# A ring of six weight blocks and four landing buffers instead of seven and two, and adaLN work moved by a step

## The chip, the cores and the metric

The kernel runs on one core of a Trainium2 chip. The metric is the device time of one execution in microseconds, the median over runs. The core has these engines, each with its own queue that it works through in order: TensorE (PE, matmuls; PEld are its weight loads), VectorE (DVE), ScalarE (ACT), GpSimd (POOL) and SyncE (SP, which here only issues loads and stores). Data comes from HBM by DMA into SBUF; matmul results land in PSUM.

## The reference

Two layers of a diffusion backbone on 384 tokens of width 1024 (256 latent, 128 context), all in float32. A layer is a half-step SwiGLU feed-forward, a token mixing stage, and a second half-step feed-forward:

```python
x = x + 0.5 * post(swiglu(pre(x, 0), gate1, up1, down1), 0)
y = token_mix(pre(x, 1), ...)   # w_mix_in, four head groups, w_mix_out
x = x + post(y, 1)
x = x + 0.5 * post(swiglu(pre(x, 2), gate2, up2, down2), 2)
# pre(y, i)  = rms_norm(y) * norm_pre  * (1 + scale_i) + shift_i
# post(y, i) = gate_i * rms_norm(y) * norm_post
# shift, scale, gate = columns of silu(cond) @ w_ada + b_ada   (9 vectors of 1024 a layer, for two conds)
```

The token mixing projects to 2560 columns, which four groups share: a gated convolution of width 3 (A), differential attention (B), a convolution of width 31 with layer norm (C), and grouped-query attention with q/k norm (D). Their outputs go through one output projection.

## The kernel before, in words

**Precision by three products.** Each float32 operand is split into a high part (rounded to fp32r) and a low part (the rest), and a product is made of three matmuls: high by high, high by low, low by high (`mm3_a`, `mm3_b`, and the three in `rows_out`, L576 to L578). The third-order product is left out.

**The weight stream.** All weights but w_ada are packed on the host into 322 blocks of 128 x 1024 (one of 128 x 512), in the order of their use. The class `Stream` brings them in. `load` issues a block's DMA from SyncE into a landing buffer (`st`, pool `sp`, `STAGES` buffers). `pump` splits the next block: a cast by ScalarE (L167) into the high half of a ring slot (`wu`, pool `up`, `UNITS` slots), and a subtraction by VectorE (L168) into the low half; this frees the landing buffer, and `pump` asks for loads up to `STAGES` blocks ahead. `take(n)` hands out the next n blocks, and first pumps up to `first + UNITS`, `first` being the first block taken; with `ahead=False` it pumps only what it takes; `tick` pumps one more. A slot is free again when TensorE has read its block for the last time.

**The stages.** `ffn` first projects one or two column groups with tokens as rows (`take(4)`, `proj_b`, bank `ps_gu`; in the very first call in four quarters, together with the first adaLN), turns them by transposes (`ps_ht`), then loops over the other column groups with features as rows (two `take(2)` a step, 48 matmuls of 128x384 each, `ps_f`), and ends in `rows_out`: 22 down-projection blocks, 18 matmuls of 128x512 a block, the last `TAIL` = 4 taken together so that one token tile after the other finishes. Behind each token tile come the norms of `post` and of the next stage's `pre` (`xn`, transposes `ps_t`). `mix` begins with `take(4)` for group C, `take(4)` for group D (followed by `d_rows`, a chain of VectorE and GpSimd work for each token tile), then attention units with fill work between them: the first fill is `take(4, False)` for q and k of group B.

**adaLN.** The columns of shift, scale and gate for later stages are computed inside `ffn` by the class `Ada`, one object for 1024 columns (a unit). Its eight steps each load 128 rows of w_ada (`ast`, pool `ap_`, 2 buffers) and add them, weighted, to two accumulators on VectorE (L275, L279). `finish` then sums over partitions by ones-matmuls (`ps_ada`, L291); for shift and scale ScalarE copies the sums to `rows` (L297) and TensorE transposes them (`ps_mod`, L300); for a gate GpSimd loads bias and norm rows and writes the result out. The closure `more` in `ffn` makes the steps: at each half of a column group `max(len(adas) * ADA_J, 0.5)` of them, in `rows_out` at every second block so many that all are done by block `ADA_END`, where `more(100)` does what is left. The first call has six units, the others 4, 5 and 1.

**What sets the order.** The program is written in one order; a planner of the framework then lays out each engine's queue, by that order and by when it reckons that an operation's inputs are there. So matmuls of a later line can stand ahead of a transpose, and loads run ahead of the line that they are written in. On the chip each queue is worked through in order, with waits.

Of the kernel before, what the change touches and what calls it, by code (L numbers as in the profile page):

```python
# [12 lines left out]
F32 = mybir.dt.float32  # L13
# [6 lines left out]
P = 128  # L20
D = 1024
KC = D // P
# [7 lines left out]
CK = 31  # L30
CPAD = CK // 2
SK = 3
UNITS = 7
STAGES = 2
TAIL = 4
MOD_DVE = (2, 0)
ORDERS = ((0, 1, 2), (0, 1, 2))
# [7 lines left out]
NORM_GAP = 2  # L45
FIRST_T = 1
ADA_J = 0.28
ADA_END = 18
CONV1 = 4
A_STEPS = 11  # L50
MIX_ORDER = (6, 7, 0, 1, 4, 5, 2, 3)
# [135 lines left out]
def kernel(ctx: ExitStack, tc: tile.TileContext, a: dict):  # L187
    nc = tc.nc
# [19 lines left out]
    def mbank(name):  # L208
        return psp.tile([P, 512], F32, tag="msc", name=name, bufs=2)
# [3 lines left out]
    def nm(s):  # L213
        uid[0] += 1
        return f"{s}{uid[0]}"
# [41 lines left out]
    class Ada:  # L257


        def __init__(self, l, i, m):  # L260
            self.key = (l, i)
            self.m = m
            self.src = a["w_ada"][l, :, (3 * i + m) * D : (3 * i + m + 1) * D]
            self.k = 0

        def step(self, pool):
            k = self.k
            w = ap_.tile([P, D], F32, tag="ast", name=nm("ast"))
            nc.sync.dma_start(out=w, in_=self.src[k * P : (k + 1) * P, :])
            if k == 0:  # L270
                self.acc = [pool.tile([P, D], F32, tag="acc", name=nm("acc"), bufs=2) for _ in range(2)]
            for c in range(2):
                s1 = sc[:, k, 0, c : c + 1]
                if k == 0:
                    nc.vector.tensor_scalar(  # L275
                        out=self.acc[c], in0=w, scalar1=s1, scalar2=None, op0=ALU.mult
                    )
                else:
                    nc.vector.scalar_tensor_tensor(  # L279
                        out=self.acc[c], in0=w, scalar=s1, in1=self.acc[c], op0=ALU.mult, op1=ALU.add  # L280
                    )
            self.k += 1
            return self.k == KC

        def finish(self):
            l, i = self.key
            ps = mbank(nm("ps_ada"))
            for c in range(2):
                for h in range(2):
                    j = 2 * c + h  # L290
                    nc.tensor.matmul(  # L291
                        ps[32 * j : 32 * j + 32, :], lhsT=ones, rhs=self.acc[c][:, h * 512 : (h + 1) * 512],
                        start=True, stop=True, tile_position=(0, 32 * j),
                    )
            if self.m < 2:
                rows = tp.tile([P, 512], F32, tag="t2k", name=nm("rows"), bufs=4)
                nc.scalar.copy(out=rows, in_=ps)  # L297
                pt = mbank(nm("ps_mod"))
                for q in range(4):
                    nc.tensor.transpose(  # L300
                        pt[:, q * P : (q + 1) * P], rows[:, q * P : (q + 1) * P], ident
                    )
                if self.m == 0:
                    raws[(l, i)] = sm.tile([P, 2, KC, 2], F32, tag="mraw", name=nm("mraw"), bufs=2)
                raw = raws[(l, i)]
                pv = pt.rearrange("p (q c h r) -> p h q c r", q=4, c=2, h=2)
                for h in range(2):
                    nc.vector.tensor_copy(
                        out=raw[:, self.m, 4 * h : 4 * h + 4, :], in_=pv[:, h, :, :, 0]
                    )  # L310
                if self.m == 1:
                    A, B = modulation(l, i, raws.pop((l, i)), 0, KC)
                    mods[(l, i)] = [(A[:, 4 * q : 4 * q + 4], B[:, 4 * q : 4 * q + 4]) for q in range(2)]
            else:
                br = tp.tile([P, 512], F32, tag="t2k", name=nm("brow"), bufs=4)
                pr = tp.tile([P, 512], F32, tag="t2k", name=nm("prow"), bufs=4)
                for j in range(4):
                    h = j % 2
                    nc.gpsimd.dma_start(
                        out=br[32 * j : 32 * j + 32, :],  # L320
                        in_=a["b_ada"][l, (3 * i + 2) * D + h * 512 : (3 * i + 2) * D + (h + 1) * 512].partition_broadcast(32),
                    )
                    nc.gpsimd.dma_start(
                        out=pr[32 * j : 32 * j + 32, :],
                        in_=a["norm_post"][l, i, h * 512 : (h + 1) * 512].partition_broadcast(32),
                    )
                grow = tp.tile([P, 512], F32, tag="grow", name=nm("grow"))
                nc.vector.tensor_tensor(out=br, in0=br, in1=ps, op=ALU.add)
                nc.vector.scalar_tensor_tensor(  # L329
                    out=grow, in0=br, scalar=(1.0 if i == 1 else 0.5), in1=pr, op0=ALU.mult, op1=ALU.mult  # L330
                )
                held = []
                for c in range(2):
                    d = dp.tile([D], F32, tag=f"gd{c}", name=nm("gd"))
                    for h in range(2):
                        r = 32 * (2 * c + h)
                        nc.gpsimd.dma_start(  # L337
                            out=d[h * 512 : (h + 1) * 512].unsqueeze(0), in_=grow[r : r + 1, :]
                        )
                    held.append(d)  # L340
                grows[(l, i)] = held

    raws = {}
    mods = {}
# [258 lines left out]
    def ffn(l, i, h, adas, nxt, first=None):  # L603
# [27 lines left out]
        with tc.tile_pool(name=nm("fp"), bufs=1) as fp:  # L631
            hid = fp.tile([P, FC, TOK], F32, name=nm("hid"))
            j0 = 1 if first is None else 2
            nb = 256 * j0
            for t in range(NT):
                pg, pu = gus[t]
                sg = tp.tile([P, 512], F32, tag="t2k", name=nm("sg"), bufs=4)
                nc.scalar.activation(out=sg[:, 0:nb], in_=pg[:, 0:nb], func=AF.Silu)
                nc.vector.tensor_tensor(out=sg[:, 0:nb], in0=sg[:, 0:nb], in1=pu[:, 0:nb], op=ALU.mult)
                pt = mbank(nm("ps_ht"))  # L640
                for q in range(2 * j0):
                    nc.tensor.transpose(pt[:, q * P : (q + 1) * P], sg[:, q * P : (q + 1) * P], ident)
                nc.vector.tensor_copy(
                    out=hid[:, 0 : 2 * j0, t * P : (t + 1) * P],
                    in_=pt[:, 0:nb].rearrange("p (q n) -> p q n", n=P),
                )

            done = []

            def more(n):  # L650
                while done:
                    done.pop(0).finish()
                rate[0] += n
                while fill and rate[0] >= 1:
                    f = fill.pop(0)
                    rate[0] -= 1
                    if f.step(fp):
                        done.append(f)
                        if n < 100:
                            break  # L660
                        done.pop(0).finish()

            for j in range(j0, FC // 2):
                if first is not None and j == 3:
                    setup_rest()
                gu = []
                for _ in range(2):
                    more(max(len(adas) * ADA_J, 0.5))
                    us = W.take(2)
                    ps = [bank(nm("ps_f")) for cc in range(2)]  # L670
                    for cc in range(2):
                        proj_a(ps[cc][:, 0:TOK], h, us, cc)
                    gu.append(ps)
                sg = tp.tile([P, 2, TOK], F32, tag="t4k", name=nm("sg"))
                for cc in range(2):
                    nc.scalar.activation(out=sg[:, cc, :], in_=gu[0][cc][:, 0:TOK], func=AF.Silu)  # L676
                    nc.vector.tensor_tensor(  # L677
                        out=hid[:, 2 * j + cc, :], in0=sg[:, cc, :], in1=gu[1][cc][:, 0:TOK], op=ALU.mult
                    )
            load_gates(l, i)  # L680
            cache = {}

            def lhs(f):
                pr = f // 2
                if pr not in cache:
                    more(100 if f >= ADA_END else len(fill) / ((ADA_END - f) / 2))
                    q = hp.tile([P, 2, 2, TOK], F32R, tag="hc", name=nm("hid_s"))
                    split_pair(q, slice(0, TOK), hid[:, 2 * pr : 2 * pr + 2, :])
                    cache[pr] = q
                return cache[pr], f % 2  # L690

            return rows_out(l, i, lhs, range(FC), nxt)
# [579 lines left out]
```

## Time and profile before

| | |
|---|---|
| median of 3 runs | 1563.77 us (1561.25 to 1564.76) |
| the profiled execution | 1562.17 us, its span 1560.4 us |
| TensorE busy | 1500.0 us, 96 % |
| VectorE busy | 1050.7 us, 67 % |
| ScalarE busy | 633.7 us, 41 % |
| GpSimd busy | 126.4 us, 8 % |
| mean DMA rate | 167 GB/s |
| granted clock, mean | 0.986 |

All times in the rows are microseconds from the start of the span, except means marked ns. An instruction is shown as engine, line of the kernel, operation, output<-inputs by the program's names. The page's busy time of TensorE counts pipelined matmuls from start to modelled end, so stalls inside a pipeline can hide in it.

### The profile page before, as it was taken

What the parts mean: (1) busy time and instruction counts of PE and PEld (TensorE: products, weight loads), DVE (VectorE), ACT (ScalarE), POOL (GpSimd) and SP (SyncE); (2) the same over time, 40 slices, a digit from 0 to 9 for tenths busy, and PEclk for the clock granted to TensorE, in tenths of its full rate; (3) what the DMA queues carried; (4) which work ended last, traced back from release to release, by engine and by line L of the source; (5) the groups of instructions that cost most, each with busy time, mean ns of one, the idle gap of its engine ahead of it and who ended that gap; (6) DMA issues with size and microseconds to landing.
All of it is one profiled execution on the core that took longest, in us unless ns stands there. A gap on an engine that the chain in (4) does not pass through costs nothing. (4 is left out here: it accounts for less than half of the span.)

```text
span 1560.4 us, 20661 instructions
## 1 busy us (share of the span) xinstructions
PE 1500.0 (96%) x7924; PEld 1319.9 (85%) x7924; DVE 1050.7 (67%) x1454; ACT 633.7 (41%) x1103; POOL 126.4 (8%) x234
## 2 busy tenths in 40 slices
PE   6899999999999999999999999999999999999997
PEld 3699998776887899998879999887768879999885
DVE  3678879867887845677586766984788796333432
ACT  3442233263466632334263333434545764323331
POOL 1101000021001201000021000002100120000000
PEclk9999999998999999999999999999999999999998
DMA  8668767733224555675546656773322245444431
GB/s 307 227 222 261 236 211 236 245 109 98 68 70 145 150 177 179 212 233 172 189 150 215 206 188 200 231 234 110 112 73 92 72 160 175 134 132 138 135 122 41
DMA packets 73619, 260.13 MB, mean 167 GB/s; under 512 B 9728, under 2 KB 9856, under 8 KB 73520
## 3 DMA queue, kind: packets, MB, share of 16 engines
q1 hardware_dynamic: 68112, 246.32, 48.5%
q0 software_dynamic: 4976, 11.70, 2.7%
q8 instruction: 62, 1.02, 0.3%
q10 hardware_dynamic: 432, 0.79, 0.1%
q14 instruction: 37, 0.30, 0.1%
HBM read 256.36 MB, written 2.41 MB: 166 GB/s over the span
## 5 line engine op out<-in xcount | busy, mean ns | idle before, releaser
L168 DVE TENSOR_TENSOR wu<-st,wu 128x1024 fp32r<-128x1024 f32 x322 | 391.6, 1219 | 296.5 <-ACT wu L167 295.9
L167 ACT CAST wu<-st 128x1024 fp32r<-128x1024 f32 x322 | 337.0, 1050 | 585.4 <-DMA st<-ws 253.7
L549 PE MATMUL ps_f<-h,wu 128*128 128x384 f32 x1248 | 418.6, 335 | 0.0
L548 PE MATMUL ps_f<-h,wu 128*128 128x384 f32 x1248 | 418.4, 336 | 0.0
L550 PE MATMUL ps_f<-h,wu 128*128 128x384 f32 x1248 | 418.3, 335 | 0.0
L279 DVE SCALAR_TENSOR_TENSOR acc<-ast,sc,acc 128x1024 f32<-128x1024 f32 x224 | 281.6, 1281 | 27.5 <-DMA ast<-w_ada 26.9
L548 PEld LDWEIGHTS ps_f<-h,wu 128*128 128x128 f32 x1248 | 234.9, 188 | 7.8 <-issue 4.2
L550 PEld LDWEIGHTS ps_f<-h,wu 128*128 128x128 f32 x1248 | 235.0, 188 | 0.0
L549 PEld LDWEIGHTS ps_f<-h,wu 128*128 128x128 f32 x1248 | 235.0, 188 | 0.0
L576 PE MATMUL ps_o<-wu,hid_s 128*128 128x512 f32 x528 | 206.5, 391 | 0.0
L577 PE MATMUL ps_o<-wu,hid_s 128*128 128x512 f32 x528 | 206.0, 390 | 0.0
L578 PE MATMUL ps_o<-wu,hid_s 128*128 128x512 f32 x528 | 205.5, 389 | 0.0
L576 PEld LDWEIGHTS ps_o<-wu,hid_s 128*128 128x128 f32 x528 | 99.1, 188 | 26.1 <-issue 5.9
L578 PEld LDWEIGHTS ps_o<-wu,hid_s 128*128 128x128 f32 x528 | 99.1, 188 | 20.6
L577 PEld LDWEIGHTS ps_o<-wu,hid_s 128*128 128x128 f32 x528 | 99.1, 188 | 20.0
L543 PE MATMUL ps_j<-wu,h 128*128 128x512 f32 (+1 forms) x192 | 73.1, 381 | 5.3 <-DVE wu L168 5.3
L542 PE MATMUL ps_j<-wu,h 128*128 128x512 f32 (+1 forms) x192 | 74.5, 388 | 0.0
L544 PE MATMUL ps_j<-wu,h 128*128 128x512 f32 (+1 forms) x192 | 72.6, 378 | 0.0
L676 ACT ACTIVATE sg<-ps_f 128x384 f32<-128x384 f32 x78 | 38.0, 487 | 83.4 <-PE ps_f L550 79.3
L799 DVE SCALAR_TENSOR_TENSOR cacc<-upad,late,cacc 128x399 f32<-128x399 f32 x120 | 69.9, 630 | 0.0
L337 POOL DMA_DIRECT2D gd<-grow x24 | 11.7, 496 | 676.0 <-DVE grow L329 676.0
L677 DVE TENSOR_TENSOR hid<-sg,ps_f 128x384 f32<-128x384 f32 x78 | 42.9, 549 | 23.3 <-PE ps_f L550 23.3
(234 smaller groups left out, 1701.0 us busy)
## 6 DMA issues: line engine op xcount, KB each, us to landing
st<-ws SPq DMA_DIRECT2D x320, 512.0 KB, 3.9
ast<-w_ada SPq DMA_DIRECT2D x128, 512.0 KB, 4.4
a<-ada SPq DMA_DIRECT2D x16, 512.0 KB, 9.3
G<-gd POOLq DMA_DIRECT2D x12, 512.0 KB, 4.7
brow<-b_ada POOLq DMA_DIRECT2D x24, 64.0 KB, 5.6
prow<-norm_post POOLq DMA_DIRECT2D x24, 64.0 KB, 6.1
x<-x_sample SPq DMA_DIRECT2D x2, 512.0 KB, 5.2
x<-x_prompt SPq DMA_DIRECT2D x1, 512.0 KB, 8.9
```

The source lines that it names most:

```text
L167: nc.scalar.copy(out=u[:, 0, :], in_=x)
L168: nc.vector.tensor_tensor(out=u[:, 1, :], in0=x, in1=u[:, 0, :].bitcast(F32), op=ALU.subtract)
L279: nc.vector.scalar_tensor_tensor(out=self.acc[c], in0=w, scalar=s1, in1=self.acc[c], op0=ALU.mult, op1=ALU.add)
L542: nc.tensor.matmul(out, lhsT=hk(h, k, 0, tsl), rhs=wh, start=start, stop=False)
L543: nc.tensor.matmul(out, lhsT=hk(h, k, 0, tsl), rhs=wl, start=False, stop=False)
L544: nc.tensor.matmul(out, lhsT=hk(h, k, 1, tsl), rhs=wh, start=False, stop=stop)
L548: nc.tensor.matmul(out, lhsT=wh, rhs=hk(h, k, 0, sl), start=start, stop=False)
L549: nc.tensor.matmul(out, lhsT=wh, rhs=hk(h, k, 1, sl), start=False, stop=False)
L550: nc.tensor.matmul(out, lhsT=wl, rhs=hk(h, k, 0, sl), start=False, stop=stop)
L576: nc.tensor.matmul(out, lhsT=pr[:, 0, s, tsl], rhs=u[:, 0, hsl], start=(q == 0), stop=False)
L577: nc.tensor.matmul(out, lhsT=pr[:, 0, s, tsl], rhs=u[:, 1, hsl], start=False, stop=False)
L578: nc.tensor.matmul(out, lhsT=pr[:, 1, s, tsl], rhs=u[:, 0, hsl], start=False, stop=(q == n - 1))
```

## The change

`UNITS` goes from 7 to 6 and `STAGES` from 2 to 4: the ring loses one slot of 8 KB a partition, and the landing buffers gain two of 4 KB. `Ada.step` no longer loads its own rows: a new method `load` issues the next load of the unit, at most one step beyond the coming one, and `more` calls it before a step and, for the next unit in line, after it. `finish` returns after the copy to `rows`; the transposes and what follows them become a method `turn`, which `more` calls at its next call, or at once in `more(100)`. `ADA_END` goes from 18 to 16.

```diff
-UNITS = 7
-STAGES = 2
+UNITS = 6
+STAGES = 4
-ADA_END = 18
+ADA_END = 16
 class Ada:
+        def load(self, pool):
+            if self.n == KC or self.n > self.k + 1:
+                return
+            w = pool.tile([P, D], F32, tag="ast", name=nm("ast"))
+            nc.sync.dma_start(out=w, in_=self.src[self.n * P : (self.n + 1) * P, :])
+            self.n += 1
+            self.w.append(w)
         def step(self, pool):
             k = self.k
-            w = ap_.tile([P, D], F32, tag="ast", name=nm("ast"))
-            nc.sync.dma_start(out=w, in_=self.src[k * P : (k + 1) * P, :])
+            w = self.w.pop(0)
...
         def finish(self):
...
             if self.m < 2:
-                rows = tp.tile([P, 512], F32, tag="t2k", name=nm("rows"), bufs=4)
-                nc.scalar.copy(out=rows, in_=ps)
-                pt = mbank(nm("ps_mod"))
-                for q in range(4):
-                    nc.tensor.transpose(
-                        pt[:, q * P : (q + 1) * P], rows[:, q * P : (q + 1) * P], ident
-                    )
...
+                self.rows = tp.tile([P, 512], F32, tag="t2k", name=nm("rows"), bufs=4)
+                nc.scalar.copy(out=self.rows, in_=ps)
+                return True
...
+        def turn(self):
+            l, i = self.key
+            pt = mbank(nm("ps_mod"))
+            for q in range(4):
+                nc.tensor.transpose(
+                    pt[:, q * P : (q + 1) * P], self.rows[:, q * P : (q + 1) * P], ident
+                )
...
             def more(n):
+                while turns:
+                    turns.pop(0).turn()
                 while done:
-                    done.pop(0).finish()
+                    f = done.pop(0)
+                    if f.finish():
+                        turns.append(f)
                 rate[0] += n
                 while fill and rate[0] >= 1:
                     f = fill.pop(0)
                     rate[0] -= 1
-                    if f.step(fp):
+                    f.load(ap_)
+                    last = f.step(fp)
+                    if fill:
+                        fill[0].load(ap_)
+                    if last:
                         done.append(f)
                         if n < 100:
                             break
-                        done.pop(0).finish()
+                if n >= 100:
+                    while done:
+                        f = done.pop(0)
+                        if f.finish():
+                            f.turn()
```

## Rows read from the trace of the kernel before

**Rows 1.** The page, busy time and share of the span, TensorE.
```profile
PE 1500.0 (96%) x7924; PEld 1319.9 (85%) x7924; DVE 1050.7 (67%) x1454; ACT 633.7 (41%) x1103; POOL 126.4 (8%) x234
```

**Rows 2.** TensorE's waits: who waited for whom, us in total, times, longest.
```profile
PE ps_t L501 <- DVE xn L491: 12.1, 15, 1.3
PE ps_j L543 <- DVE wu L168: 5.3, 2, 2.6
PE ps_ht L642 <- DVE sg L639: 4.6, 1, 4.6
PE ps_mod L300 <- ACT rows L297: 4.2, 3, 1.6
```

**Rows 3.** Stretches after four stalls; after POOL stands the granted clock (PEclk).
```profile
75.60:80.70 5.10, 5.05 (x18) 5.08 (x19) 4.26 (x7) 3.15 (x5) 0.00 (x0) 0.50 0.66 198
...
163.50:168.50 5.00, 4.98 (x30) 4.98 (x31) 3.95 (x6) 0.49 (x1) 0.00 (x0) 1.00 0.78 244
...
378.30:387.90 9.60, 9.60 (x21) 6.33 (x22) 9.37 (x16) 2.77 (x4) 0.00 (x0) 0.50 0.49 155
...
1135.60:1142.20 6.60, 6.60 (x13) 4.10 (x14) 6.60 (x12) 2.70 (x4) 0.00 (x0) 0.50 0.50 169
```

**Rows 4.** The same view over the column groups of a feed-forward.
```profile
540.00:780.00 240.00, 240.00 (x1293) 224.16 (x1293) 149.38 (x151) 79.80 (x92) 7.64 (x16) 1.00 0.61 195
```

**Rows 5.** Timeline of all engines before the 4.6 us stall: start, duration.
```profile
59.67 0.62 POOL L420 DMA_DIRECT2D lqp<-diff_lq  x1 [44.58 <-DVE h L465]
...
60.58 1.42 SPq L156 DMA_DIRECT2D st<-ws  x2
...
69.07 1.05 ACT L167 CAST wu<-st 128x1024 fp32r<-128x1024 f32 x1 [5.67 <-DMA st<-ws]
...
70.02 0.59 ACT L638 ACTIVATE sg<-ps_gu 128x512 f32<-128x512 f32 x1
...
74.82 0.68 DVE L639 TENSOR_TENSOR sg<-sg,ps_gu 128x512 f32<-128x512 f32 x1
```

**Rows 6.** SyncE's issues from 45 to 58 us.
```profile
45.16 0.90 SPq L269 DMA_DIRECT2D ast<-w_ada  x2
49.97 4.92 SPq L156 DMA_DIRECT2D st<-ws  x2
```

**Rows 7.** Timeline of ScalarE before the first wait of `ps_mod`.
```profile
161.94 1.04 ACT L167 CAST wu<-st 128x1024 fp32r<-128x1024 f32 x1 [1.65 <-DMA st<-ws]
162.89 0.58 ACT L297 COPY rows<-ps_ada 128x512 f32<-128x512 f32 x1
```

**Rows 8.** Timeline in the mixing stage of layer 0, q and k of group B.
```profile
373.09 0.39 PE L543 MATMUL ps_j<-wu,h 128*128 128x512 f32 x1
...
375.29 0.40 PE L542 MATMUL ps_j<-wu,h 128*128 128x512 f32 x1
...
377.03 2.36 DVE L168 TENSOR_TENSOR wu<-st,wu 128x1024 fp32r<-128x1024 f32 x2
```

**Rows 9.** Timeline at the entry to the second feed-forward of layer 0.
```profile
521.00 0.39 PE L543 MATMUL ps_gu<-wu,h 128*128 128x512 f32 x1
...
521.47 1.22 DVE L168 TENSOR_TENSOR wu<-st,wu 128x1024 fp32r<-128x1024 f32 x1
...
522.59 0.65 PE L543 MATMUL ps_gu<-wu,h 128*128 128x512 f32 x2
...
523.95 1.22 DVE L168 TENSOR_TENSOR wu<-st,wu 128x1024 fp32r<-128x1024 f32 x1
```

**Rows 10.** Timeline at the entry to the mixing stage of layer 0.
```profile
331.65 2.35 DVE L168 TENSOR_TENSOR wu<-st,wu 128x1024 fp32r<-128x1024 f32 x2
...
334.14 0.39 PE L543 MATMUL ps_j<-wu,h 128*128 128x512 f32 x1
```

**Rows 11.** Timeline at the end of the first feed-forward's adaLN work.
```profile
303.03 2.48 DVE L279 SCALAR_TENSOR_TENSOR acc<-ast,sc,acc 128x1024 f32<-128x1024 f32 x2 [0.62 <-DMA ast<-w_ada]
...
309.21 1.07 PE L291 MATMUL ps_ada<-acc,ones 128*32 128x512 f32 x8
```

More of the change, by code (lines that the diff above doesn't have):

```diff
@@ L264, in __init__ @@
             self.k = 0
+            self.n = 0
+            self.w = []
+        def load(self, pool):
[5 more added lines that the diff above has]
+            self.w.append(w)
         def step(self, pool):
             k = self.k
-            w = ap_.tile([P, D], F32, tag="ast", name=nm("ast"))
-            nc.sync.dma_start(out=w, in_=self.src[k * P : (k + 1) * P, :])
+            w = self.w.pop(0)
             if k == 0:
@@ L295, in finish @@
             if self.m < 2:
-                rows = tp.tile([P, 512], F32, tag="t2k", name=nm("rows"), bufs=4)
-                nc.scalar.copy(out=rows, in_=ps)
-                pt = mbank(nm("ps_mod"))
-                for q in range(4):
-                    nc.tensor.transpose(
-                        pt[:, q * P : (q + 1) * P], rows[:, q * P : (q + 1) * P], ident
-                    )
[L303 to L313, printed above, removed]
+                self.rows = tp.tile([P, 512], F32, tag="t2k", name=nm("rows"), bufs=4)
+                nc.scalar.copy(out=self.rows, in_=ps)
+                return True
             else:
@@ L341, in finish @@
                 grows[(l, i)] = held
+                return False
+        def turn(self):
[5 more added lines that the diff above has]
+                )
+            if self.m == 0:
+                raws[(l, i)] = sm.tile([P, 2, KC, 2], F32, tag="mraw", name=nm("mraw"), bufs=2)
+            raw = raws[(l, i)]
+            pv = pt.rearrange("p (q c h r) -> p h q c r", q=4, c=2, h=2)
+            for h in range(2):
+                nc.vector.tensor_copy(
+                    out=raw[:, self.m, 4 * h : 4 * h + 4, :], in_=pv[:, h, :, :, 0]
+                )
+            if self.m == 1:
+                A, B = modulation(l, i, raws.pop((l, i)), 0, KC)
+                mods[(l, i)] = [(A[:, 4 * q : 4 * q + 4], B[:, 4 * q : 4 * q + 4]) for q in range(2)]
     raws = {}
@@ L646, in ffn @@
                 )
-            done = []
+            done, turns = [], []
             def more(n):
+                while turns:
+                    turns.pop(0).turn()
                 while done:
-                    done.pop(0).finish()
+                    f = done.pop(0)
+                    if f.finish():
+                        turns.append(f)
                 rate[0] += n
```

## The prediction

> **What bounds the kernel now.** I read the busy shares first, then TensorE's waits, then a table of stretches with the granted clock, and last the timeline around each wait. TensorE is busy for 96 % of the span [rows 1], and in the long feed-forward stretch from 540 to 780 us it has no idle time at all: 240.00 of 240.00 us [rows 4]. Whatever VectorE, ScalarE and the loads wait for in such a stretch costs nothing. So an edit can move the time in two ways only: by the stalls of TensorE that it removes, and by new ones at the places where a weight block comes just in time. The removable ones stand in the waits of TensorE [rows 2]: 4.6 us once for `sg` before the transposes `ps_ht`, 4.2 us in three waits of the transposes `ps_mod` for the copied rows, 5.3 us in two waits for a weight block's low half, and 12.1 us in 15 waits for `xn`, which is the norm's own chain of operations and which nothing here shortens.
>
> [...]
>
> **Four landing buffers.** Block b's load is issued when a landing buffer is free, so behind the split of block b-2 before and of b-4 after. Where a block is read long after its split this is worth nothing. It is worth something where ScalarE, which works in order, stands at a cast whose data has not landed while TensorE waits for what is queued behind. There are two such places.
>
> First, the start. Blocks 10 and 11 are issued from 60.58, beside four small broadcasts that GpSimd issues from 59.67 on; the cast waits 5.67 us and starts at 69.07, so the load took some 8.5 us, where the page's median is 3.9. The `sg` activation runs right behind it at 70.02, VectorE's `sg` at 74.82, and TensorE has waited 4.61 us [rows 5]. With four buffers these two loads take the places that blocks 8 and 9 have now, 49.97 to 54.9 [rows 6], and at 3.9 us each they are down before the broadcasts start. Blocks 12 and 13, which the cast then reaches, follow the splits of 8 and 9; with data no longer late these can run in the idle time around 50 us, again ahead of 59.67. So I take the whole stall, 4.6 us, and half of the 5.10 us at half clock, 2.55: a gain of 7.2. Bounds: 0 (another cast stands there instead) to 7.2.
>
> [...]
>
> Second, the three waits of `ps_mod`. At 161.94 a cast starts after 1.65 us of waiting for its load, and the copy of the adaLN rows starts only at 162.89 behind it [rows 7]; TensorE waits for that copy. Loads that are four blocks ahead take this wait away.
>
> **Rows transposed one step later.** The four transposes leave the place right behind the column sums and stand behind the next 48 matmuls, some 8 us on, when the copy (0.58 us [rows 7]) is long done. This removes the same three waits a second time; only the last adaLN unit of a call keeps its old order. Together I take 4.2 us, bounds 2.6 (the longest one, 1.6, stays, being that of a last unit) and 4.2; their stalls left the clock at 1.00. The work itself is the same and nothing reads the result for tens of us.
>
> **adaLN columns a step ahead.** The pool for these columns keeps its two buffers, and the trace has two of their loads issued at 45.16 [rows 6], long before the first sum at 57.6. They are already issued when a buffer is free. I cost this at nothing: behind them SyncE's queue holds weight loads which have now more room, and TensorE is covered [rows 4]. Bounds minus 1 to plus 1.
>
> **adaLN done by block 16 instead of 18.** The first feed-forward call has six units, and there VectorE is late: the last sum ends at 303.03 + 2.48 = 305.5, and TensorE's column-sum matmul stands at 309.21, where the tail begins [rows 11]. Two blocks earlier are 36 matmuls of 0.227 us, 8.2 us, so 301.0. If it stands there, TensorE waits up to 4.5 us; if it is placed by readiness, 0. VectorE's work for later steps can be pushed back, so I take 1.0.
>
> **Six weight blocks instead of seven.** This speaks against the change. A call that takes four blocks for its first projection finds three of them split in advance now, and two afterwards, because `take` runs ahead only to the first held block plus the ring's size. The third block moves to the next `take`, behind everything that the program writes in between, and inherits the place in VectorE's queue that the fourth has now. The split itself costs the same; what counts is whether the fourth's place is too late for the third.
>
> In the mixing stage (twice) it is. The third block's low half is read at 373.09, the fourth's after 375.29 + 0.23; the fourth's split is done first in a pair that starts at 377.03 and so at 378.25 [rows 8]. TensorE then stands from 373.1 instead of 375.5, 2.4 us more. But the half-clock stretch would begin that much earlier too, and up to 1.2 us come back. I take 1.5 each, 3.0 in all; bounds 0 (other matmuls are put in between) and 3.9 each (2.4, and a stretch of 9.6 us instead of 6.6, half of 3.0).
>
> At the three calls of a feed-forward that follow another stage's output (516, 805 and 1275 us have the same pattern) the third block is read at 521.00 and would be ready at 521.47 + 1.22 = 522.69; the fourth is read from 522.59 on and would come at 523.95 + 1.22 = 525.17 [rows 9]. That is 1.7 us, then 0.9, 2.6 in all. A little later TensorE waits for `xn` anyhow, 0.8 us on average [rows 2], and 1.7 us of lateness lets this wait go. I take 1.2 each, 3.6; bounds 0 and 2.6.
>
> At the two entries to the mixing stage the pair is split from 331.65, the first done at 332.87, and the third block's low half is read at 334.14 [rows 10]: 1.3 us to spare, so 0.
>
> **Sum.** Gains 7.2 + 4.2 = 11.4, losses 3.0 + 3.6 + 1.0 = 7.6: 3.8 us off. The profiled execution took 1562.17 us (1560.4 of span and 1.8 around it), so 1558.4; the median of the runs lies 1.6 above it, so 1560.0.
>
> **Rivals.**
> The ring decides (slower). At the three feed-forward calls the 1.7 and 0.9 us come close together, and in sum they are as long as the 2.6 us stalls that were followed by half clock [rows 3]. If each is, it costs 2.6 and half of 6.6 us, so 5.9, three times 17.7; with 4.0 elsewhere and 11.4 of gains: 10.3 slower, 1574. It decides once the five places together lose over 11.4 us. For it: nothing else in VectorE's queue moves there. Against: `x2` in the row at 522.59 shows that matmuls of the next token tile are already put between. [...]
>
> The start stall stays: blocks 14 and 15, or the adaLN column, meet the broadcasts and hold up ScalarE or VectorE. Then 7.2 are missing: 1567.2. For it: the broadcasts do not move. Against: those blocks' casts wait for TensorE to release a ring slot after `sg`.
>
> The ring costs nothing, since the order is planned anew around it: losses 1.0 alone, 1553.4. For it: the `x2`; against: at 373 to 378 us TensorE found nothing to put in.
>
> **How the numbers follow.** Forecast 0.45 (its own range 1556 to 1564), the ring decides 0.15, the start stall stays 0.22, the ring costs nothing 0.18. The range 1553 to 1570 reaches to the middle of the third and to the fourth and leaves out the far part of the second. What a measurement can tell from no change is 0.2 %, 3.1 us: under 1560.6 is faster, over 1566.9 slower. Faster: a little over half of the forecast and all of the fourth, 0.43. Slower: the second and half of the third, and a trace of the first, 0.28. The rest, 0.29, is the same.
>
> **What would show it.** `ps_ht` <- `sg` gone from TensorE's waits and 1.00 in the clock at 75 us; no `ps_mod` <- `rows`; in the mixing stages a wait for `wu` of about 5 us instead of 2.6; new waits for `wu` near 521, 805 and 1275 us, below 2 us; ScalarE's casts waiting for TensorE and hardly for loads. I am wrong if the first is still there, if the clock falls to 0.50 at the feed-forward calls, or if a wait of `ps_ada` for `acc` appears near 301 us.

## The result, and the profile after

The kernel after takes 1544.59 us (median of 4 runs, 1543.18 to 1548.72) beside 1564.26 for the kernel before on the same chip: ratio 0.988 with a 95 % interval of 0.9859 to 0.990. I had forecast 1560.0 and a range from 1553 to 1570. The sign was right; the gain is 19.7 us instead of 3.8.

The profiled run is the slowest of the four, 1548.72 us with a span of 1546.9. Its engine shares, beside [rows 1]:

```profile
PE 1492.0 (96%) x7924; PEld 1312.3 (85%) x7924; DVE 1048.2 (68%) x1454; ACT 635.4 (41%) x1103; POOL 131.4 (8%) x234
```

TensorE runs the same 7924 matmuls. It is busy for 8.0 us less and idle for 5.5 us less (60.4 before, 1546.9 - 1492.0 = 54.9 now). The three half-clock stretches of [rows 3], 21.3 us together at a granted clock of 0.50 and so by my estimate worth some 10.6 us, are gone (below). By this estimate more than half of the 13.5 us that the trace gained is half clock that no longer follows a stall. TensorE's waits, beside [rows 2]:

```profile
PE ps_t L515 <- DVE xn L505: 14.9, 14, 2.7
...
PE ps_dT L873 <- DVE dr L757: 3.4, 2, 1.7
...
PE ps_gu L556 <- ACT h L478: 1.7, 4, 0.6
...
PE ps_gu L557 <- DVE wu L168: 1.3, 3, 0.6
```

The waits of `ps_ht` for `sg` and of `ps_mod` for the adaLN rows are gone, as forecast. The wait of `ps_j` for `wu`, which I had expected to double, is gone too; in its place `ps_dT` waits 1.7 us in each mixing stage for `dr`. The stretches beside [rows 3, 4], with the granted clock in the third column from the right:

```profile
74.00:82.00 8.00, 8.00 (x48) 8.00 (x48) 8.00 (x8) 4.00 (x5) 2.06 (x5) 1.00 0.97 213
374.00:388.00 14.00, 13.93 (x71) 10.33 (x70) 14.00 (x28) 5.76 (x17) 0.00 (x0) 1.00 0.11 39
413.50:417.10 3.60, 3.60 (x13) 3.59 (x14) 3.15 (x7) 0.63 (x3) 0.00 (x0) 0.53 0.28 113
...
540.00:780.00 240.00, 240.00 (x1281) 221.22 (x1280) 153.71 (x156) 76.86 (x90) 11.46 (x20) 1.00 0.59 190
785.60:789.20 3.60, 3.60 (x11) 2.78 (x9) 3.60 (x8) 3.54 (x11) 0.62 (x1) 0.53 0.06 20
1130.00:1143.00 13.00, 12.94 (x67) 9.56 (x66) 13.00 (x25) 5.34 (x15) 0.00 (x0) 1.00 0.13 42
```

The three half-clock stretches of before are at 1.00. Of the two short ones the first stands at the same work as one of before (0.53 from 425.4 to 429.0 us there); the second is new. By stages, from the first matmul of a stage's first block to that of the next (us, profiled executions; the last column is the run land4_again below):

| stage | before | after | forecast | measured | buffers alone |
|---|---|---|---|---|---|
| start and first feed-forward | 331.2 | 324.8 | -10.4 | -6.4 | 322.8 |
| mixing, layer 0 | 185.2 | 178.7 | +1.5 | -6.4 | 175.3 |
| mixing, layer 1 | 182.8 | 176.1 | +1.5 | -6.7 | 175.9 |
| the three other feed-forwards | 861.2 | 867.3 | +3.6 | +6.1 | 865.2 |
| span | 1560.4 | 1546.9 | -3.8 | -13.5 | 1539.3 |

In the mixing stages I expected 3.0 us of loss and found 13.1 of gain. By these two executions the error is 9.7 us (13.5 gained instead of 3.8): 16.1 in the mixing stages, less 4.0 at the start and 2.5 in the later feed-forwards. The error of the medians, 15.9, is larger because the profiled execution after lies 4.1 us above its median and the one before 2.1 below. Of the 13.1 us, 10.2 lie in q and k of group B, which take 33.3 and 33.2 us in the two layers where they took 38.8 and 38.0.

Why, is best seen from SyncE's line that loads the blocks: how many loads, who waited for them (us, times), and how long they took. First before, then after:

```profile
L156 SPq DMA_DIRECT2D st<-ws x322: 327/328/1224, 4.7 to 1514.5; - x161
...
  ACT wu L167: 253.7, 107
...
DMA to landing us min/median/max: 2.4/3.9/13.3
```

```profile
L156 SPq DMA_DIRECT2D st<-ws x322: 327/328/1117, 5.2 to 1497.0; - x161
...
  ACT wu L167: 0.2, 1
...
DMA to landing us min/median/max: 2.6/4.3/14.4
```

The loads are not faster; their median even rises from 3.9 to 4.3 us. But before, 107 of the 322 casts stood waiting for one, 253.7 us in all; now one does, for 0.2 us. ScalarE's casts now wait for TensorE to free a ring slot instead: 266.4 us for `ps_f` and 206.7 for `ps_o`, where it was 170.6 and 139.8.

What this did in the mixing stage stands in the timelines of ScalarE and VectorE (start, duration, instruction, in brackets the idle time ahead of it and what ended it). Before, while group D of layer 0 is projected, ScalarE and then VectorE:

```profile
355.09 1.05 ACT L167 CAST wu<-st 128x1024 fp32r<-128x1024 f32 x1 [1.92 <-DMA st<-ws]
356.04 0.37 ACT L770 COPY upad<-ps_uT 128x256 f32<-128x256 f32 x1
```

```profile
356.17 1.23 DVE L168 TENSOR_TENSOR wu<-st,wu 128x1024 fp32r<-128x1024 f32 x1 [2.81 <-ACT wu L167]
357.31 0.88 DVE L794 TENSOR_SCALAR cacc<-upad,late 128x399 f32<-128x399 f32 x2
358.11 1.22 DVE L168 TENSOR_TENSOR wu<-st,wu 128x1024 fp32r<-128x1024 f32 x1
359.24 0.55 DVE L814 TENSOR_REDUCE ss<-sqd 128x6 f32<-128x384 f32 x1
...
373.82 0.63 DVE L799 SCALAR_TENSOR_TENSOR cacc<-upad,late,cacc 128x399 f32<-128x399 f32 x1
```

And VectorE after:

```profile
343.59 3.77 DVE L168 TENSOR_TENSOR wu<-st,wu 128x1024 fp32r<-128x1024 f32 x3 [0.71 <-ACT wu L167]
...
348.04 1.23 DVE L168 TENSOR_TENSOR wu<-st,wu 128x1024 fp32r<-128x1024 f32 x1 [0.35 <-ACT wu L167]
350.03 0.89 DVE L820 TENSOR_SCALAR cacc<-upad,late 128x399 f32<-128x399 f32 x2 [0.76 <-ACT upad L796]
350.83 2.27 DVE L825 SCALAR_TENSOR_TENSOR cacc<-upad,late,cacc 128x399 f32<-128x399 f32 x4
353.01 0.55 DVE L840 TENSOR_REDUCE ss<-sqd 128x6 f32<-128x384 f32 x1
...
360.81 0.63 DVE L825 SCALAR_TENSOR_TENSOR cacc<-upad,late,cacc 128x399 f32<-128x399 f32 x1
...
364.03 1.22 DVE L168 TENSOR_TENSOR wu<-st,wu 128x1024 fp32r<-128x1024 f32 x1
...
366.17 1.22 DVE L168 TENSOR_TENSOR wu<-st,wu 128x1024 fp32r<-128x1024 f32 x1
```

TensorE after, at the low halves of the third and the fourth block:

```profile
368.60 0.39 PE L557 MATMUL ps_j<-wu,h 128*128 128x512 f32 x1
...
371.03 0.39 PE L557 MATMUL ps_j<-wu,h 128*128 128x512 f32 x1
```

The program writes twelve convolution steps (`cacc`, `CONVD` = 4 for each of three token tiles) ahead of the splits for q and k. Before, ScalarE stands for 1.92 us at a cast whose load is late; behind it are the last copy to `upad`, which these steps read, and VectorE's split, for which VectorE idles 2.81 us. That split, the third block's and only two steps are done when the chain `d_rows` of the first token tile begins (`ss`, 359.24). The other ten steps fill the gaps of the three chains up to 373.82, and the fourth block's split comes after the last chain, at 377.03 [rows 8]. After, the split at 348.04 is the last one ahead of the steps (the third block has no slot yet: its cast starts at 359.19, when `ps_j` has freed one); six steps are done before the first chain, and the twelfth runs at 360.81. So the splits of the third and fourth block (364.03, 366.17) find room in the gaps of the second chain, and each is done 3.3 us or more ahead of the matmul that reads its low half (368.60 and 371.03). These orders are the planner's. The traces show the order; what the planner reckoned with is not on record.

### The profile page after: what moved, and what is told of

It is laid out like the page before. It is cut to its first block, busy times and chain, and to the rows that moved or that the text cites. A ratio compares the mean times of both kernels' runs of the same rounds, so it can differ in the third digit from the quotient of the medians.

```text
span 1546.9 us, 20700 instructions
## 1 busy us (share of the span) xinstructions
PE 1492.0 (96%) x7924; PEld 1312.3 (85%) x7924; DVE 1048.2 (68%) x1454; ACT 635.4 (41%) x1103; POOL 131.4 (8%) x234
## 5 line engine op out<-in xcount | busy, mean ns | idle before, releaser
L167 ACT CAST wu<-st 128x1024 fp32r<-128x1024 f32 x322 | 337.1, 1052 | 536.2 <-PE ps_f L564 266.4
L556 PE MATMUL ps_j<-wu,h 128*128 128x512 f32 (+1 forms) x192 | 72.8, 379 | 0.0
L558 PE MATMUL ps_j<-wu,h 128*128 128x512 f32 (+1 forms) x192 | 70.5, 367 | 1.1 <-DVE h L479 1.1
L557 PE MATMUL ps_j<-wu,h 128*128 128x512 f32 (+1 forms) x192 | 69.8, 363 | 0.0
## 6 DMA issues: line engine op xcount, KB each, us to landing
a<-ada SPq DMA_DIRECT2D x16, 512.0 KB, 10.2
x<-x_prompt SPq DMA_DIRECT2D x1, 512.0 KB, 10.6
```

The source lines that it names most:

```text
L167: nc.scalar.copy(out=u[:, 0, :], in_=x)
L556: nc.tensor.matmul(out, lhsT=hk(h, k, 0, tsl), rhs=wh, start=start, stop=False)
L557: nc.tensor.matmul(out, lhsT=hk(h, k, 0, tsl), rhs=wl, start=False, stop=False)
L558: nc.tensor.matmul(out, lhsT=hk(h, k, 1, tsl), rhs=wh, start=False, stop=stop)
```

## The experiments

Each set of four ran on one chip beside the kernel before (1565.69 us in the first set, 1561.38 in the second, 1564.68 in the third). Theory A: the two extra landing buffers make all of the gain. Rivals: the adaLN edits make part of it (B); the smaller ring by itself lets the planner order the mixing stage better (C). In the second set: what held the split back in the mixing stage.

**First set: the parts apart.** ring6_land4 is the kernel before with the buffer edit alone:

```diff
-UNITS = 7
-STAGES = 2
+UNITS = 6
+STAGES = 4
```

> The kernel before with six ring slots and four landing buffers, adaLN code as before. Theory A (the landing buffers decide: a block's data is there earlier, so its split gets an earlier place in VectorE's queue, in the mixing stage too): 12 to 17 us faster, some 1547 to 1552; TensorE's wait of 2.6 us for wu in each mixing stage is gone, no half-clock stretch at 75, 378 and 1135 us. Theory B (the adaLN edits changed the planned order, and the gain in the mixing stage is theirs): at most 7 us faster by the start, with waits for wu of about 5 us in both mixing stages.

Measured: 1543.5 us, ratio 0.9852 (0.9834 to 0.987). Neither of the removed waits is there, nor the wait for `wu` in the mixing stages. The buffer edit alone makes the whole gain, 22.2 us, more than the 12 to 17 that I had expected.

ring6_land2 takes the slot away and gives no landing buffer:

```diff
-UNITS = 7
+UNITS = 6
```

> The kernel before with six ring slots, still two landing buffers. Theory A: the price of the smaller ring as it was predicted, waits for wu of about 5 us instead of 2.6 in each mixing stage and new ones at the feed-forward entries, 3 to 8 us slower, 1567 to 1572; the 4.6 us wait for sg at 75 us stays. Theory C (the smaller ring itself lets the planner order the mixing stage better): 5 us faster or more, and no wait for wu in the mixing stage.

Measured: 1570.14 us, ratio 1.0023 (1.0009 to 1.0037). TensorE's waits:

```profile
PE ps_dT L847 <- DVE dn L831: 7.6, 2, 3.8
PE ps_mod L300 <- ACT rows L297: 5.3, 4, 3.4
PE ps_ht L642 <- DVE sg L639: 4.4, 1, 4.4
```

```profile
380.37 2.35 DVE L168 TENSOR_TENSOR wu<-st,wu 128x1024 fp32r<-128x1024 f32 x2
```

The third block's split now starts at 380.37, behind the last `d_rows`, the place that I had forecast for it. But TensorE waits elsewhere than I had said: it stands at the transposes of that same chain (`dn`) for 3.8 us a stage, where it stood 2.6 for `wu`; I had taken 5 for `wu`, of which there is none in the mixing stages. Beside before, the two mixing stages of the profiled executions are 2.0 us shorter and 3.2 longer, and the three later feed-forwards 5.0 longer in sum. By the ratio the run is some 3.6 us slower where I had priced the ring at 6.6. So for two landing buffers the place was read rightly and the size only roughly. C falls, since the run is slower.

ada_edits_only is the kernel after with the old buffers:

```diff
-UNITS = 6
-STAGES = 4
+UNITS = 7
+STAGES = 2
```

> The change with seven ring slots and two landing buffers, so the adaLN edits alone. Theory A: 2 to 4 us faster (1560 to 1562) by the three waits of ps_mod, waits for wu in the mixing stages and for sg at the start as before. Theory B: 10 us faster or more, and the waits for wu in the mixing stages gone.

Measured: 1563.53 us, ratio 0.999 (0.9975 to 1.0005). B falls.

```profile
PE ps_j L557 <- DVE wu L168: 5.2, 2, 2.6
PE ps_ht L656 <- DVE sg L653: 3.7, 1, 3.7
PE ps_ada L300 <- DVE acc L288: 2.5, 1, 2.5
```

Theory A's 2 to 4 us are not seen either. No `ps_mod` wait for adaLN rows of a later stage is left: the later transposes do remove these waits by themselves. But `ADA_END` = 16 brings the wait of `ps_ada` for `acc` that I had named as a sign of error, and takes back about what that gained.

ring6_land3 has six slots and three landing buffers:

```diff
-UNITS = 7
-STAGES = 2
+UNITS = 6
+STAGES = 3
```

> The kernel before with six ring slots and three landing buffers. Theory A: between the runs with two and four; if one more buffer is enough for the place in VectorE's queue, the mixing stage's waits for wu are gone and it is within 4 us of the run with four. Theory C: like the run with two landing buffers.

Measured: 1550.83 us, ratio 0.9895 (0.9876 to 0.9915). The third buffer brings most of the gain: `ps_ht` waits 0.5 us, and the waits of `ps_mod` for the adaLN rows are gone. It brings it at the start: the start and first feed-forward take 320.2 us, but the mixing stages still take 182.6 and 181.0. The fourth removes two waits of 2.5 us for `kTg` in the mixing stages (the mean granted clock is 0.990 with three and 0.995 with four), and so most of the mixing stages' gain is the fourth's. I had said within 4 us of the run with four; it is 7.3.

**Second set: the mechanisms.** broadcasts_late is the kernel before with GpSimd's small loads written later:

```diff
-                if first is not None and j == 3:
+                if first is not None and j == 6:
```

> The kernel before (seven slots, two landing buffers), with GpSimd's small broadcasts (`setup_rest`) issued three column groups later (j == 6 instead of 3), so that they no longer stand beside the loads of blocks 10 and 11. Theory of the prediction (the 8.5 us load is slow because the broadcasts are in flight beside it): the 4.6 us wait of `ps_ht` for `sg` is gone or under 1 us, the granted clock is 1.00 from 74 to 80 us, and the time is 5 to 8 us below before, 1557 to 1560. Rival (two landing buffers are too few for the cast order there, with or without broadcasts): the wait stays at 3.5 us or more, and the time is within 2 us of before.

Measured: 1562.96 us, ratio 1.0015 (0.9999 to 1.0031). The planner moved them only from 59.67 to 70.85, and put an adaLN load of GpSimd in their old place. The loads of blocks 10 and 11 took 5.4 and 5.6 us instead of 8.5 and 8.9, and the stall shrank from 4.6 to 1.5. The time did not. Waits and stretches:

```profile
PE ps_mod L300 <- ACT rows L297: 7.1, 3, 4.1
...
PE ps_ht L642 <- DVE sg L639: 1.5, 1, 1.5
```

```profile
72.00:80.00 8.00, 6.58 (x40) 6.61 (x41) 5.55 (x8) 3.39 (x5) 1.03 (x2) 1.00 0.91 245
161.00:168.00 7.00, 6.60 (x25) 6.61 (x26) 5.98 (x8) 0.36 (x2) 0.00 (x0) 0.58 0.79 269
```

The first `ps_mod` wait grew from 1.6 to 4.1 us, and the low clock now stands there (0.58 from 161 to 168 us, 1.00 from 72 to 80). So these two loads were shorter with the broadcasts moved away, as the prediction had it, though the adaLN load that took their place keeps the run from showing this alone. With two landing buffers the stream is late elsewhere too (from 120 to 165 us nine waits of casts for their loads, 28.9 us in all), and what the stall lost in one place came back at the next: taking it away gave nothing here.

conv_later_land2 is the kernel before without convolution steps written between the token tiles of group D:

```diff
-CONVD = 4
+CONVD = 0
```

> The kernel before (seven slots, two landing buffers) with CONVD = 0 instead of 4: the convolution steps that VectorE does between the token tiles of group D are done later, in the attention part. It tells why the fourth block's split came late in the mixing stage. Backlog theory (VectorE is late there because the convolution steps stand ahead of the split): the 2.6 us waits of TensorE for `wu` in the two mixing stages are gone or under 1 us, the clock stays 1.00 there, and q and k of group B take about 33 us instead of 38. Readiness theory (the split has its place in VectorE's queue behind the last `d_rows` because the planner reckons the block to land late with two landing buffers): the wait stays between 1.5 and 3 us, since `d_rows` alone stands ahead. The total is not forecast closer than 1558 to 1572, as the convolution has to be done later.

Measured: 1562.19 us, ratio 1.0002 (0.9985 to 1.0019). VectorE:

```profile
369.88 0.62 DVE L799 SCALAR_TENSOR_TENSOR cacc<-upad,late,cacc 128x399 f32<-128x399 f32 x1
...
373.09 1.22 DVE L168 TENSOR_TENSOR wu<-st,wu 128x1024 fp32r<-128x1024 f32 x1
...
375.23 1.22 DVE L168 TENSOR_TENSOR wu<-st,wu 128x1024 fp32r<-128x1024 f32 x1
```

Only seven convolution steps now stand ahead of the fourth block's split (twelve before). It takes a gap of the second chain, as it does after, and no wait for `wu` is left in the mixing stages: the backlog theory. The readiness theory (the split comes late because its load does) falls here, since the loads are as late as before (VectorE idles 2.83 us ahead of the split at 359.54, 2.81 ahead of that at 356.17 before). Of the 10.2 us that q and k gain in the change, only 4.1 came: they take 35.7 and 36.9 us, not 33, because `ps_dT` then waits 3.2 us for `dr` and `ps_s` 2.1 for `kTg`; and this was lost elsewhere (the start and first feed-forward take 3.4 us more in the profiled execution).

conv_more_land4 is ring6_land4 with more of them:

```diff
-CONVD = 4
+CONVD = 8
```

> Six slots, four landing buffers, adaLN as before (as in the run ring6_land4), with CONVD = 8 instead of 4: VectorE does 12 more convolution steps of about 0.57 us, 6.8 us in all, between the token tiles of group D. Backlog theory: the splits of the third and fourth block of q and k move back by several us, TensorE waits for `wu` again in the mixing stages (over 1 us each), and the total is 3 to 8 us above that of ring6_land4, 1547 to 1552. Readiness theory: the splits keep their place ahead of the last `d_rows`, no wait for `wu` over 1 us, 1541 to 1546.

Measured: 1569.06 us, ratio 1.0058 (1.0037 to 1.0079), where ring6_land4 has 0.9852. VectorE:

```profile
368.60 3.90 DVE L799 SCALAR_TENSOR_TENSOR cacc<-upad,late,cacc 128x399 f32<-128x399 f32 x7
372.41 2.35 DVE L168 TENSOR_TENSOR wu<-st,wu 128x1024 fp32r<-128x1024 f32 x2
```

With four landing buffers and all blocks landed in time (the casts of blocks 76 and 77 start at 356.4 and 357.8, as in ring6_land4), the splits are again behind the last chain and seven convolution steps, and `ps_dT` waits 3.8 us for `dn` in each stage (not for `wu`, as I had said). The direction is that of the backlog theory; the size was missed. I had said 3 to 8 us, and the two mixing stages alone are 26.9 longer than in ring6_land4 (191.4 and 187.5 us against 176.2 and 175.8), stalls and half clock together: the granted clock is 0.66 from 364 to 372 and 0.80 from 372 to 384.

ring5_land6 moves one more slot:

```diff
-UNITS = 7
-STAGES = 2
+UNITS = 5
+STAGES = 6
```

> Five ring slots and six landing buffers (the same memory), adaLN as before. If landing buffers are what counts and the ring has room to spare, it is within 3 us of ring6_land4: 1541 to 1547. If the ring now decides at the calls that take four blocks (one block split in advance instead of two), TensorE waits for `wu` at the ffn entries over 1.5 us each and in the mixing stages, with half clock behind: 1550 to 1570.

Measured: 1554.64 us, ratio 0.9963 (0.9946 to 0.9979). No cast of blocks 8 to 65 starts within 0.3 us of its load's landing, as with four buffers (before, 40 of 58 do), so the last two landing buffers find no late load to cure, while the sixth slot is missed: each of the three later feed-forwards is longer than in ring6_land4 by 1.4 to 2.9 us, the start and first one by 2.1, the mixing stages by 1.4 and 3.4, and `ps_gu` waits 5.7 us in five waits for `h`. The waits for `wu` that I had named stay small (0.6): the lateness shows at another operand.

**Third set: what the adaLN edits cost, and a better version.** after_again is the kernel after, unchanged; after_end18 has one constant back; land4_again is ring6_land4 again; land4_conv2 is that with `CONVD` = 2:

```diff
-ADA_END = 16
+ADA_END = 18
```

> The kernel after, beside the three others of this set on one chip: ratio to before 0.986 to 0.990. If the adaLN edits cost something once there are four landing buffers (the 2.2 us stall with half clock at 784 us of its first profile, which the run with the buffers alone does not have), it is 2 to 6 us above land4_again; if they cost nothing, within 2 us of it.

> The kernel after with ADA_END = 18 as before; the loads ahead and the later transposes stay. If the earlier end is what leaves VectorE late in the tail of the second feed-forward (stall of 2.2 us for `xn` at 784 us, half clock behind), the stall is under 1.5 us here, the clock stays 1.00, and the time is 2 to 5 us below after_again. If not, the stall stays and the time is within 1.5 us of after_again.

> Six slots, four landing buffers, adaLN as before, a second time, as the baseline of this set: ratio to before 0.984 to 0.987, 1541 to 1545.

> Six slots, four landing buffers, adaLN as before, with CONVD = 2 instead of 4: six convolution steps fewer (3.4 us of VectorE) between the token tiles of group D. Backlog theory: they are done before the first `d_rows`, the splits of blocks 76 and 77 move up by a gap of `d_rows` (to 358 to 361 us, from 361.3 and 363.4), the 1.7 us wait of `ps_dT` for `dr` in each mixing stage shrinks under 1 us, and the time is 1 to 3 us below land4_again if the steps find idle VectorE time in the attention part; the steps that have to be done there can take the gain back, then it is within 1.5 us. Readiness theory: the splits stay where they are, the wait too, and the time is the same or up to 3 us longer.

Measured: after_again 1544.47 us (0.9874, 0.9859 to 0.9889), after_end18 1542.24 (0.986, 0.9845 to 0.9875), land4_again 1541.27 (0.9859, 0.984 to 0.9877), land4_conv2 1542.97 (0.9865, 0.985 to 0.9879). The intervals overlap, so the 3.2 us between after_again and land4_again are a likely cost of the adaLN edits, not a firm one. By stages after_again is 1.4 us longer at the start, 1.6 in the first mixing stage and 1.1 in the second feed-forward. Of these the trace names the last one's place, its tail:

```profile
781.96 1.06 PE L515 MATMUL ps_t<-early,xn 128*128 128x128 f32 x8 [1.95 <-DVE xn L505]
```

With `ADA_END` = 18 no wait for `xn` there is above 0.9 us, and the median is 2.2 us lower. In land4_conv2 I was wrong: its splits stand where they were (362.3 and 364.5 us, 362.1 and 364.2 in land4_again), as the readiness theory had said. The same twelve convolution steps stand ahead of them in both runs, those of later lines in place of the six taken away, so the edit did not change what it was to change and does not tell the theories apart. In both runs the two splits start 3.8 and 4.6 us after their casts are done, with VectorE idle for 1.5 us in between. Why the planner places them there is open.

land4_again beats the kernel before by 23.4 us and has the lowest median of all versions run; after_end18 and land4_conv2 lie within its interval. Whether seven slots with three or four landing buffers would be better was not tried: they need 4 or 8 KB more a partition.

## Why the prediction was wrong

**The step that failed** is in the part on the ring: "The third block moves to the next `take` [...] and inherits the place in VectorE's queue that the fourth has now." I took that place as given by the program, where it was the result of a backlog on VectorE (conv_later_land2, conv_more_land4), and the backlog goes with the landing buffers that are the other half of the change (ring6_land4 against ring6_land2). The parts were priced one by one against the trace of before. For the ring alone the place was right: with two landing buffers the third block does inherit it. With four, VectorE has the convolution steps behind it early, both splits are in time, and each mixing stage loses its 2.6 us stall and the half clock behind it instead of paying more. That is 6.4 and 6.7 us of gain where I had 1.5 of loss each. In q and k this accounts for the size: 2.6 us of stall and half of 9.6 and of 6.6 us (an estimate from the granted clock of 0.50 there), less the new wait of 1.7, make 5.7 and 4.2, and 5.5 and 4.7 were measured. What gives the other 2.9 us in the mixing stages was not traced. No rival had a gain there, so that even the lowest of them (1553.4) lies 8.8 us above the measured time. That it is the late loads that make the backlog is read from the timelines; no run moves the loads alone.

**The sign was in the profile of before.** The 253.7 us that ScalarE waited for loads stand in the waits of ScalarE, and I set such waits aside because TensorE is covered in the feed-forwards. They are covered there [rows 4], but in the mixing stage they become VectorE's 2.81 us of idling and then a late split. Two landing buffers leave 107 casts waiting, and going to three and four, with six slots, gave ratios of 0.9895 and 0.9852.

**The start stall**, 7.2 us: right. `ps_ht` no longer waits, the clock is 1.00 from 74 to 82 us, and the first 48 matmuls of `ps_f` with what stands among them take 8.9 us instead of 16.1. One step on the way was not: blocks 12 and 13 are issued at 60.7 and 62.6, not around 50; the broadcasts moved too, to 63.50, and these loads took 4.4 and 5.0 us. Blocks 14 and 15, which the second rival named, do meet the broadcasts and take 7.8 and 7.9 us, and blocks 16 and 17, issued at 74.5 and 76.2 beside GpSimd's adaLN loads, 8.3 and 8.1, where the median of all is 4.3. What makes these four long was not taken apart; blocks 14 to 17 are cast 4.6 us or more after landing, and nobody waits.

**The three `ps_mod` waits**, 4.2 us: gone. Both edits remove them, each without the other (ring6_land4, ada_edits_only), as I had said; so the second one has nothing left to gain.

Of these two terms' 11.4 us, less 1.0, the trace shows 6.4 up to the mixing stage; 1.8 of what is missing is the beginning, where the first adaLN columns landed later (TensorE starts at 14.12 us instead of 12.36) in this execution. In land4_again it is 8.4. What remains is a price that I had not seen: the opening quarters of the first feed-forward. Their first matmul and the first of `ps_f`, before and then after:

```profile
21.03 0.79 PE L542 MATMUL ps_gu<-wu,h 128*128 128x512 f32 x1 [0.55 <-ACT h L464]
...
67.47 0.42 PE L548 MATMUL ps_f<-h,wu 128*128 128x384 f32 x1
```

```profile
22.81 0.79 PE L556 MATMUL ps_gu<-wu,h 128*128 128x512 f32 x1 [0.55 <-ACT h L478]
...
71.98 0.42 PE L562 MATMUL ps_f<-h,wu 128*128 128x384 f32 x1
```

That is 46.4 and 49.2 us for the same 144 matmuls and what stands among them. All runs with two or three landing buffers take 45.8 to 46.6 us, all with four 48.5 to 49.5, and ring5_land6 50.2. In these quarters the first adaLN's matmuls (`ps_first`), which stand in 6 or 7 groups there, stand in 11 with four or six. Whether the loads of the blocks, now further ahead, hold up those of the adaLN columns was not tested.

**adaLN columns ahead**, 0: nothing speaks against it, but it was not tried alone.

**`ADA_END`**, 1.0 with bounds 0 to 4.5: the size is within the bounds (2.2 by the medians of after_end18 and after_again, whose intervals overlap), the place was not right. No wait of `ps_ada` for `acc` is left with four buffers; VectorE's lateness shows in the tail of the second feed-forward (`ps_t` waits 1.95 us for `xn` in after_again).

**The feed-forward entries**, 3.6 us with bounds 0 and 7.8 for all three: the three stages are 6.1 longer, and 4.0 with the buffers alone. The waits for `wu` are 0.6 or less each. The rival that put half clock behind them did not come: the losses stay small and apart, and the granted clock is 1.00 from 505 to 525, from 794 to 812 and from 1258 to 1275 us. At the mixing entries groups C and D take 0.3 us more, for which I had 0.

## What to carry to other kernels

Before pricing a part against the old trace, ask whether another part of the same change moves the queue that the price is read from: here the late place of a split in VectorE's queue was a symptom, and the buffers that ended ScalarE's wait upstream (253.7 us before, 0.2 after) changed the places behind it. Count how often the first engine of a weight stream waits for its load: 107 times of 322 here before, once after. Here the cure was depth of landing buffers, and the removal of a single stall (broadcasts_late) gave nothing. When memory is fixed, time some ways to share it between ring slots and landing buffers: 6 slots and 4 buffers was the best of those run (1543.5 and 1541.27 us), and both 7 and 2 (1561.38 to 1565.69) and 5 and 6 (1554.64) were longer. Look at the opening too: its quarters took 2.7 us longer with four landing buffers (46.4 and 49.2).

## What was not expected of the hardware

Of two stalls of about 2 us at the same place, one was followed by half clock and one was not. The 2.03 us wait at 784.42 us in the first profile of the kernel after was followed by 3.6 us at a granted clock of 0.53; the same wait of 1.95 us at 781.96 in the second profile by none (1.00 from 781 to 790 us). By an estimate from the 0.53 over 3.6 us, that is 1.7 us between two executions of one kernel.

Nor did a low clock cost time everywhere. From 21 to 28 us, in the opening, the granted clock is 0.64 in ring6_land4 and 1.00 in land4_again, the same kernel on another chip; from its first `ps_gu` matmul to the mixing stage the first takes 300.9 us and the second 301.1.
